# Sums of squares as pairs of float32r products, one product turned into a transposition, and a first weight tile loaded ahead of x

## Chip, cores and metric

The kernel runs as one program on one core of a Trainium2 chip. The metric is the device time of one execution in microseconds (us); a kernel is judged by the median of its runs.

## What is computed

One step of a two-layer decoder trunk for 1024 prompt rows and 64 sample rows (8 sequences of 8), side by side as 1088 columns. Layer 0 mixes by a gated delta rule (GDN, 4 heads) and a latent attention (8 heads); layer 1 by a gated linear recurrence (HGRN2, 8 heads of 128). Every mixer and every MLP is preceded by an RMS norm, and the mixers normalise per head. These are the places at which sums of squares are taken:

```
def rmsnorm(x, g):                      # over 1024 before each mixer, each MLP and at the end;
    xf = x.astype(jnp.float32)          # over 128 on each head's output
    y = xf * lax.rsqrt(jnp.mean(xf * xf, axis=-1, keepdims=True) + EPS)
    return (y * g.astype(jnp.float32)).astype(x.dtype)

def l2norm(x):                          # on q and k of each GDN head
    xf = x.astype(jnp.float32)
    return xf * lax.rsqrt(jnp.sum(xf * xf, axis=-1, keepdims=True) + EPS)
...
x = x + o
x = x + sq_relu_mlp(rmsnorm(x, mlp_norm[layer]), w_up[layer], w_down[layer])
```

## The kernel before, in words

Activations stand transposed: features on 128 partitions, the 1088 rows as columns, in three chunks of 384, 384 and 320 (`CH`). Every large product is made of three float32r products (`dense`, L335 to L337): weights and activations are each split into a high part, the value cast to float32r, and a low part, the rest (`split_pair`, L265 the cast on ACT, L266 the subtraction on DVE); high by high, high by low and low by high are added up in PSUM. Small products run on plain float32 operands.

A sum of squares over the features is a product with a 128x128 matrix of ones (`k.ones`): it leaves the sum of a column on all partitions. It stands at these places:

- The norm over 1024 features, `split_x`, one chunk at a time: ACT squares eight 128-row tiles, POOL adds the first seven into `ssa` (L286), the eighth stays in `ssl`, and `inv_rms` makes two float32 products with ones (L295), one on each. This is done for x before layer 0, before each MLP and before layer 1; the last norm (`final_norm`) has the same two products.
- `pairs` in `in_proj`, once per GDN head: six products (L695), three chunks each of k and q, one behind the other in a small pipeline of three `nq` buffers.
- The end of `core` in `hgrn`, once per HGRN2 head: three products (L1935) on `o2`, the squares of the head's output.

`attend_prompt` brings reciprocals, one per query row, onto 64 partitions each: `rcw` times the identity, a float32 product (L1454), 32 times.

Four things set the order of the work. The Python generators are woven (`weave`): the projections of the next head run between the steps of the present one (`core(h)` with `proj(h + 1)`, and `core(7)` with `out_early`). The framework then orders the instructions of each engine when the program is built, by a time model of its own. Each engine takes its instructions strictly in that order. And tiles of one tag in one pool share a fixed number of buffers: a new tile waits until the last reader of the tile that held its buffer is done. In `hgrn` the tiles `y` of the seven levels of a head, and `kd`, share the two buffers of the tag "y". In `pairs` the tags "he" and "hd" have one buffer each; `he` takes the load of `cum_d` (L712) for each group of chunks.

At the start SP and ACT load x in pairs of 128-row tiles (`load_x`, L447), two of the four for each chunk on each queue; the first weight tile `win` (L457) follows on SP, and the constants `cst`, the ones and the identity among them.

Of the kernel before, what the change touches and what calls it, by code (L numbers as in the profile page):

```python
# [13 lines left out]
ALU = mybir.AluOpType  # L14
# [157 lines left out]
def setup(k, nc, tc, A, O, ctx):  # L172
    k.nc, k.tc, k.A, k.O, k.ctx = nc, tc, A, O, ctx
    k.P = lambda name, bufs=1, **kw: tc.tile_pool(name=name, bufs=bufs, **({} if kw.get("space") == DRAM else {"reuse_waits": "tile"}), **kw)
    k.cp = ctx.enter_context(k.P("consts"))
    k.cst = k.cp.tile([128, NCST], F32, name="cst")
    k.vec = k.cp.tile([128, NVEC], F32, name="vec")
    k.eps = k.cp.tile([128, 2], F32, name="eps")
    k.rb = k.cp.tile([128, NT], F32, name="rb")
    k.dr = ctx.enter_context(k.P("dr", space=DRAM))  # L180
    nc.scalar.preload_act_table_set(EXP_SET)
    nc.gpsimd.memset(k.eps[:, 0:1], EPS)
    nc.gpsimd.memset(k.eps[:, 1:2], EPS * 128)
    C = lambda o, n, p=128: k.cst[0:p, o:o + n]
    k.ident, k.tri, k.maskT = C(C_ID, 128), C(C_TRI, 128), C(C_MT, 128)
    k.tri8, k.mk8, k.ones, k.ones8 = C(C_TRI8, 64, 64), C(C_MK8, 64, 64), C(C_ONE, 128), C(C_ONE8, 64, 64)
    k.V = lambda o: k.vec[:, o:o + 1]
# [78 lines left out]
    (eng or k.nc.vector).tensor_tensor(lo, src, hi.bitcast(F32), ALU.subtract)  # L266


def rsqrt_from(k, out, ps, scale, bias):

    nc = k.nc
    nc.scalar.activation(out, ps, AF.Ln, bias=bias, scale=scale)
    nc.scalar.activation(out, out, AF.Exp, scale=-0.5)


def squares(k, pool, x, c, n):

    nc = k.nc
    T = lambda tag, name: pool.tile([128, 384], F32, tag=tag, bufs=2, name=name)[:, :n]
    acc = t = T("ssa", f"ssa{c}")  # L280
    for kk in range(8):
        if kk:
            t = T("ssq", f"ssq{c}{kk}") if kk < 7 else T("ssl", f"ssl{c}")
        nc.scalar.activation(t, x[:, kk], AF.Square)  # L284
        if 0 < kk < 7:
            nc.gpsimd.tensor_tensor(acc, acc, t, ALU.add)  # L286
        yield acc, t


def inv_rms(k, pool, sq, c, n, r, ps):  # L290

    nc = k.nc
    p = ps()[:, :n]
    for i in range(2):
        nc.tensor.matmul(p, k.ones, sq[i], start=i == 0, stop=i == 1)  # L295
    nc.scalar.activation(r, p, AF.Ln, bias=k.eps[:, 0:1], scale=1.0 / 1024)
    nc.scalar.activation(r, r, AF.Exp, scale=-0.5)
    yield

    v, r2 = (pool.tile([128, 384], F32, tag="nwt", bufs=2, name=f"nwt{c}{i}")[:, :n] for i in range(2))  # L300
    nc.vector.tensor_scalar(v, p, -0.5 / 1024, -0.5 * EPS, ALU.mult, ALU.add)
    nc.scalar.activation(r2, r, AF.Square)
    nc.vector.tensor_tensor(v, v, r2, ALU.mult)
    nc.vector.scalar_tensor_tensor(r, v, 1.5, r, ALU.add, ALU.mult)
    yield


def split_x(k, pool, sqp, x, c, n, g_off, r, ps, xs, lag):
# [7 lines left out]
    for kk in range(8):  # L316
        nc.scalar.mul(hi[:, kk], x[:, kk], k.V(g_off + kk))
        nc.vector.scalar_tensor_tensor(lo[:, kk], x[:, kk], k.V(g_off + kk), hi[:, kk].bitcast(F32),  # L318
                                       ALU.mult, ALU.subtract)
        sq = next(s)  # L320
        yield
    for _ in range(lag):
        yield
    yield from inv_rms(k, sqp, sq, c, n, r, ps)
# [101 lines left out]
def in_proj(k):  # L426
# [16 lines left out]
    def load_x(c):  # L443
        t0, n = CH[c]
        x = xlp.tile([128, 8, 384], F32, tag="x", bufs=2, name=f"x{c}")[:, :, :n]
        for i in range(0, 8, 2):
            (nc.scalar if i % 4 else nc.sync).dma_start(x[:, i:i + 2], A["xT"][:, i:i + 2, t0:t0 + n])  # L447
        xv.append(x)


# [8 lines left out]
    def split_next():  # L459
        if raws:  # L460
            W.append(split_w(k, xp, raws.popleft(), [128, 8, 128], "w", 2))
    nc.scalar.dma_start(k.vec, A["vec"])
    load_x(0)
    load_w(xlp, "w0")
    nc.sync.dma_start(k.cst, A["cst"])
    load_x(1)
    load_w()
# [206 lines left out]
    def pairs(h, ys, z):  # L674
# [7 lines left out]
        yield  # L682
        items = [(t, t0, n) for t in (kn, q) for t0, n in CH]
        T = lambda i: rp.tile([128, 384], F32, tag="nq", bufs=3, name=f"nq{h}{i}")[:, :items[i][2]]
        r, ps = {}, {}
        for i in range(len(items) + 2):
            if i > 1:
# [4 lines left out]
            if 0 < i <= len(items):  # L692
                n = items[i - 1][2]
                ps[i - 1] = k.mm()[:, :n]
                nc.tensor.matmul(ps[i - 1], k.ones, r[i - 1], start=True, stop=True)  # L695
            if i < len(items):
                t, t0, n = items[i]
                r[i] = T(i)
                nc.scalar.activation(r[i], t[:, t0:t0 + n], AF.Square)
            yield  # L700
        nc.sync.dma_start(k.y_d[h, 1], kn)
        egl, egs = k.egl[h], k.egs[h]
# [643 lines left out]
def attend_prompt(k):  # L1346
# [76 lines left out]
    def mix(hp, qb, Ps):  # L1423
# [27 lines left out]

        rcw = T([128, 2, 64], f"rcw{hp}{qb}", tag="rcw", bufs=2)
        nc.gpsimd.tensor_copy(rcw, Ps[0][1].unsqueeze(2).broadcast_to([128, 2, 64]))
        nc.tensor.matmul(po[:, 128:256], rcw.rearrange("p j d -> p (j d)"), k.ident, start=True, stop=True)  # L1454
        tm = T([128, 128], f"to{hp}{qb}", tag="tm", bufs=2)
        ob = T([128, 128], f"ob{hp}{qb}", tag="ob", bufs=2)
        nc.scalar.copy(tm, po[:, 128:256])
# [246 lines left out]
def hgrn(k, X, before):  # L1704
# [61 lines left out]
    def core(h):  # L1766
# [150 lines left out]
        for c in range(8):  # L1917
# [12 lines left out]
            St = Sn  # L1930
            yield 0.9
        nc.sync.dma_start(O["hgrn_p"][h], St)
        for c, (t0, n) in enumerate(CH):
            p = k.sm()
            nc.tensor.matmul(p[:, :n], k.ones, o2[:, t0:t0 + n], start=True, stop=True)  # L1935
            nc.scalar.activation(o2[:, t0:t0 + n], p[:, :n], AF.Ln, bias=epsd, scale=1.0 / 128)
        nc.scalar.activation(o2, o2, AF.Exp, scale=-0.5)
        nc.vector.tensor_tensor(oz, oz, o2, ALU.mult)
# [57 lines left out]
```

## Time and profile before

| | |
|---|---|
| Runs | 3300.77 us median of 3 (3298.63 to 3304.87) |
| Profiled execution | 3298.84 us, of which the span of its instructions is 3297.1 us |
| TensorE clock granted, mean | 0.984 of full speed |
| PE busy | 3163.4 us, 96% of the span |
| DVE busy | 1709.0 us, 52% |
| ACT busy | 1107.8 us, 34% |
| POOL busy | 543.8 us, 16% |
| DMA | 288.70 MB, mean 88 GB/s |

A busy time counts an engine from the first to the last moment of each instruction; matmuls overlap, so a busy PE may still have slack. A row of the chain of waits names the work that the end of the program hung on at that time. A float32 product shows as two MATMUL records, one of float32r as one.

### The profile page before, as it was taken

To read this page: it belongs to the slowest core of one execution; us is meant where nothing else is said; L and a number is where in the kernel's file an instruction comes from. 1 tells how busy PE (TensorE), PEld (TensorE's weight loads), DVE (VectorE), ACT (ScalarE), POOL (GpSimd) and SP (SyncE) were. 2 spreads that over 40 slices of the span, in tenths; PEclk is the share of its full clock that TensorE was granted. 3 is DMA by queue.
4 is the path that set the end of the run, shared out by engine and by line. 5 is a ranking of instruction groups with operands and counts; after the bars stand their busy time and mean duration, and the time that the engine had idled before them with its cause. 6 is when DMAs were issued, how large, how long until landed. Compare 5 with 4: busy or idle time off the path is not lost. (4 is left out here: it accounts for less than half of the span.)

```text
span 3297.1 us, 63998 instructions
## 1 busy us (share of the span) xinstructions
PE 3163.4 (96%) x26944; PEld 2928.9 (89%) x26944; DVE 1709.0 (52%) x3102; ACT 1107.8 (34%) x2046; POOL 543.8 (16%) x581
## 2 busy tenths in 40 slices
PE   8999998899989999999999999999899999999997
PEld 7777875687878999999999989889799999999997
DVE  5324443665537445444546555555656444444446
ACT  5334433344415221122123445544535122212212
POOL 3021224112102000000001344443522000000002
PEclk9999999999999999999999999999899999999999
DMA  4666668422132111111112111111322111111111
GB/s 147 199 224 202 218 225 288 149 74 94 57 115 84 45 45 42 43 52 46 33 52 77 56 53 54 53 58 43 131 73 64 33 52 52 45 33 52 46 39 55
DMA packets 140279, 288.70 MB, mean 88 GB/s; under 512 B 16536, under 2 KB 85496, under 8 KB 139992
## 3 DMA queue, kind: packets, MB, share of 16 engines
q1 hardware_dynamic: 118248, 210.60, 19.4%
q10 hardware_dynamic: 12528, 40.45, 3.8%
q0 software_dynamic: 9216, 33.56, 3.1%
q8 instruction: 212, 3.47, 0.4%
q14 instruction: 75, 0.61, 0.1%
HBM read 235.48 MB, written 49.08 MB: 86 GB/s over the span
## 5 line engine op out<-in xcount | busy, mean ns | idle before, releaser
L335 PE MATMUL mm<-xh,wh 128*128 128x384 f32 (+1 forms) x2808 | 936.9, 334 | 12.4 <-ACT wh L265 11.2
L337 PE MATMUL mm<-xh,wl 128*128 128x384 f32 (+1 forms) x2808 | 929.2, 331 | 0.2 <-DVE wl L266 0.2
L336 PE MATMUL mm<-xl,wh 128*128 128x384 f32 (+1 forms) x2808 | 929.0, 331 | 0.0
L1664 DVE TENSOR_TENSOR xr<-xr,sm 128x384 f32<-128x384 f32 (+1 forms) x768 | 404.8, 531 | 430.5 <-PE sm L1663 430.4
L335 PEld LDWEIGHTS mm<-xh,wh 128*128 128x128 f32 x2808 | 531.4, 189 | 23.3 <-ACT wh L265 11.2
L337 PEld LDWEIGHTS mm<-xh,wl 128*128 128x128 f32 x2808 | 531.0, 189 | 9.5 <-issue 6.5
L336 PEld LDWEIGHTS mm<-xl,wh 128*128 128x128 f32 x2808 | 531.0, 189 | 9.1 <-issue 5.1
L1661 PE MATMUL sm<-hh,dh 128*128 128x384 f32 (+1 forms) x1536 | 505.0, 329 | 6.6 <-DVE xr L1664 5.2
L1663 PE MATMUL sm<-hh,dl 128*128 128x384 f32 (+1 forms) x1536 | 503.2, 328 | 0.0
L1662 PE MATMUL sm<-hl,dh 128*128 128x384 f32 (+1 forms) x1536 | 502.5, 327 | 0.0
L286 POOL TENSOR_TENSOR ssa<-ssa,ssq 128x384 f32<-128x384 f32 (+1 forms) x90 | 95.1, 1057 | 1725.0 <-ACT ssq L284 1722.1
L1638 ACT ACTIVATE hraw<-hraw 128x384 f32<-128x384 f32 (+1 forms) x192 | 96.9, 505 | 689.7 <-DVE hraw L1637 689.6
L1661 PEld LDWEIGHTS sm<-hh,dh 128*128 128x128 f32 x1536 | 288.8, 188 | 9.9 <-DVE xr L1664 7.5
L1662 PEld LDWEIGHTS sm<-hl,dh 128*128 128x128 f32 x1536 | 288.6, 188 | 0.6 <-issue 0.2
L1663 PEld LDWEIGHTS sm<-hh,dl 128*128 128x128 f32 x1536 | 288.7, 188 | 0.0
L1637 DVE SCALAR_TENSOR_TENSOR hraw<-mm,rb 128x384 f32<-128x384 f32 (+1 forms) x192 | 102.7, 535 | 184.6 <-PE mm L337 184.5
L265 ACT CAST dh<-dr 128x1024 fp32r<-128x1024 f32 x64 | 66.9, 1048 | 389.6 <-PE sm L1662 381.2
L266 DVE TENSOR_TENSOR hl<-hraw,hh 128x384 fp32r<-128x384 f32 (+1 forms) x192 | 102.3, 533 | 114.8 <-ACT hh L265 114.8
L265 ACT CAST wh<-wr 128x1024 fp32r<-128x1024 f32 x96 | 100.7, 1049 | 137.2 <-PE mm L336 135.3
L266 DVE TENSOR_TENSOR wl<-wr,wh 128x1024 fp32r<-128x1024 f32 x96 | 122.3, 1275 | 37.3 <-ACT wh L265 37.2
L265 ACT CAST hh<-hraw 128x384 fp32r<-128x384 f32 (+1 forms) x192 | 94.9, 494 | 5.1
L928 POOL DMA_INDIRECT lt<-in_lat,ix x64 | 67.0, 1046 | 159.1 <-PE sc L885 66.0
(659 smaller groups left out, 4522.0 us busy)
## 6 DMA issues: line engine op xcount, KB each, us to landing
la<-in_latT SPq DMA_DIRECT2D x256, 144.0 KB, 4.2
wr<-in_w_up SPq DMA_DIRECT2D x64, 512.0 KB, 3.4
dr<-in_w_down ACTq DMA_DIRECT2D x64, 512.0 KB, 4.3
wr<-in_w_in_c SPq DMA_DIRECT2D x32, 512.0 KB, 3.5
win<-in_w_in_ab SPq DMA_DIRECT2D x21, 512.0 KB, 3.9
y_d<-y SPq DMA_DIRECT2D x12, 544.0 KB, 3.1
oC_d<-g SPq DMA_DIRECT2D x8, 544.0 KB, 3.8
q_d<-q SPq DMA_DIRECT2D x16, 256.0 KB, 3.4
```

The costliest lines, as they stand in the source:

```text
L265: k.nc.scalar.copy(hi, src)
L266: (eng or k.nc.vector).tensor_tensor(lo, src, hi.bitcast(F32), ALU.subtract)
L286: nc.gpsimd.tensor_tensor(acc, acc, t, ALU.add)
L335: nc.tensor.matmul(acc, wh[:, kk], xh, start=f, stop=False)
L336: nc.tensor.matmul(acc, wh[:, kk], xl, start=False, stop=False)
L337: nc.tensor.matmul(acc, wl[:, kk], xh, start=False, stop=l)
L1637: nc.vector.scalar_tensor_tensor(raw[:, s], p[:, :n], 0.0, k.rb[:, s], ALU.max, ALU.mult)
L1638: nc.scalar.activation(raw[:, s], raw[:, s], AF.Square)
L1661: nc.tensor.matmul(p[:, :n], wh[:, m], hh[:, s], start=a, stop=False)
L1662: nc.tensor.matmul(p[:, :n], wh[:, m], hl[:, s], start=False, stop=False)
L1663: nc.tensor.matmul(p[:, :n], wl[:, m], hh[:, s], start=False, stop=b)
L1664: nc.vector.tensor_tensor(k.xr[c][:, m], k.xr[c][:, m], p[:, :n], ALU.add)
```

## The change

It adds a float32r copy of the ones, `k.onesr`, and `col_sums`, which splits a sum of squares into two products with it: one on the high part of the squares, one on the low part. In `split_x` POOL adds the eighth square too, and the whole sum is split. In `pairs` the two parts take the buffers "he" and "hd"; in `hgrn` they take the two buffers "y", and the whole of `o2` is split at once. `final_norm` keeps its float32 products. The product with the identity becomes a transposition. At the start, the first weight tile is loaded on SP ahead of x, and all four loads of x's first chunk are on SP.

```
+    k.onesr = k.cp.tile([128, 128], F32R, name="onesr")
+    nc.gpsimd.memset(k.rb[:, 0:128], 1.0)
+    nc.gpsimd.tensor_copy(k.onesr, k.rb[:, 0:128])
...
+def col_sums(k, p, hl):
+    for i in range(2):
+        k.nc.tensor.matmul(p, k.onesr, hl[i], start=i == 0, stop=i == 1)
...
-            t = T("ssq", f"ssq{c}{kk}") if kk < 7 else T("ssl", f"ssl{c}")
+            t = T("ssq", f"ssq{c}{kk}")
...
-    for i in range(2):
-        nc.tensor.matmul(p, k.ones, sq[i], start=i == 0, stop=i == 1)
+    if sq[0] is not None:
+        for i in range(2):
+            nc.tensor.matmul(p, k.ones, sq[i], start=i == 0, stop=i == 1)
+    else:
+        col_sums(k, p, sq[1])
...
+    nc.gpsimd.tensor_tensor(sq[0], sq[0], sq[1], ALU.add)
+    yield
+    hl = [sqp.tile([128, 384], F32R, tag="ss" + i, bufs=1, name=f"ss{i}{c}")[:, :n] for i in "hl"]
+    split_pair(k, *hl, sq[0])
+    sq = None, hl
...
-            (nc.scalar if i % 4 else nc.sync).dma_start(x[:, i:i + 2], A["xT"][:, i:i + 2, t0:t0 + n])
+            (nc.scalar if i % 4 and c else nc.sync).dma_start(x[:, i:i + 2], A["xT"][:, i:i + 2, t0:t0 + n])
...
+    load_w(xlp, "w0")
     load_x(0)
-    load_w(xlp, "w0")
...
+        TR = lambda i, j: rp.tile([128, 512], F32R, tag="hd" if j else "he", bufs=1, name=f"nh{h}{i}{j}")[:, :items[i][2]]
...
-                nc.tensor.matmul(ps[i - 1], k.ones, r[i - 1], start=True, stop=True)
+                col_sums(k, ps[i - 1], hl)
...
                 nc.scalar.activation(r[i], t[:, t0:t0 + n], AF.Square)
+                hl = TR(i, 0), TR(i, 1)
+                split_pair(k, *hl, r[i])
...
-        nc.tensor.matmul(po[:, 128:256], rcw.rearrange("p j d -> p (j d)"), k.ident, start=True, stop=True)
+        nc.tensor.transpose(po[:, 128:256], rcw.rearrange("p j d -> p (j d)"), k.ident)
...
+        hl2 = [hl.tile([128, NT], F32R, tag="y", bufs=2, name=f"oh{h}{i}") for i in range(2)]
+        split_pair(k, *hl2, o2)
         for c, (t0, n) in enumerate(CH):
             p = k.sm()
-            nc.tensor.matmul(p[:, :n], k.ones, o2[:, t0:t0 + n], start=True, stop=True)
+            col_sums(k, p[:, :n], [t[:, t0:t0 + n] for t in hl2])
```

Since the order is set by the framework, the change also moves instructions that the diff does not name. Three places matter here. Line numbers of the changed kernel run ahead: L265 is L268 there, L317 is L328, L335 to L337 are L351 to L353, L1773 is L1792, L1797 is L1816, L1818 is L1837.

The first is ACT at the start, from its first load on. Before (`xh` is the high part of a tile of x, `ssa` and `ssq` are squares, `wh` the high part of the first weights):

```order
L462 DMA vec<-in_vec 128x118
L447 DMA x_91<-in_xT 128x2x384 x2
L447 DMA x_99<-in_xT 128x2x384 x2
L317 ACTIVATE xh_108<-x_91,vec 128x384
L284 ACTIVATE ssa_112<-x_91 128x384
L317 ACTIVATE xh_108<-x_91,vec 128x384
L284 ACTIVATE ssq_116<-x_91 128x384
L317 ACTIVATE xh_108<-x_91,vec 128x384
L284 ACTIVATE ssq_121<-x_91 128x384
L317 ACTIVATE xh_108<-x_91,vec 128x384 x3
L601 ACTIVATE eA<-vec 128x4
L265 CAST wh<-win 128x1024
```

And now:

```order
L478 DMA vec<-in_vec 128x118
L463 DMA x_102<-in_xT 128x2x384 x2
L268 CAST wh<-win 128x1024
L617 ACTIVATE eA<-vec 128x4
L328 ACTIVATE xh_111<-x_96,vec 128x384
L292 ACTIVATE ssa_115<-x_96 128x384
```

The cast of the first weights has moved ahead of all work on x, and two loads have left the queue.

The second is ACT between two HGRN2 heads, where the tail of head 0 and the head of head 1 overlap. `o` is head 0's output squares, `x` and `y` are head 1's level tiles, L1883 the squares of one chunk of head 0. Before:

```order
L1786 ACT_TABLE_LOAD
L1786 ACTIVATE f_21105<-f_21105,lb,om 128x1088
L201 ACT_TABLE_LOAD
L1818 COPY y_21999<-k_21950 128x544
L1883 ACTIVATE o_21593<-sm 128x128
L1817 ACTIVATE x_21998<-f_21105 128x544
L1883 ACTIVATE o_21593<-sm 128x128
```

And now, from the last square of head 0 on:

```order
L1902 ACTIVATE o_21761<-sm 128x128
L1832 ACTIVATE x_22242<-x_22242 128x1088
L268 CAST oh_22004<-o_21761 128x1088
L1837 COPY y_22174<-k_22125 128x544
L1957 ACTIVATE o_21761<-sm,epsd 128x384 x2
```

Head 1's first copy into a `y` tile stood ahead of most of head 0's squares; it now stands behind the last of them and behind the cast for head 0's sums.

The third is PE where `core(6)` begins (L1773 transposes v, L1797 and, as L1816, its successor are the 32x32 tiles of the levels). Before:

```order
L1773 MATMUL sm<-cst,v_25157 64x128
L337 MATMUL mm<-xh_20586,wl 128x320
L335 MATMUL mm<-xh_20586,wh 128x320
L336 MATMUL mm<-xl_20587,wh 128x320
L1797 MATMUL sm<-q_25154,k_26000 32x32 x34
L1797 MATMUL sm<-y_26049 32x32 x34
L1797 MATMUL sm<-y_26118 32x32 x34
L337 MATMUL mm<-xh_20586,wl 128x320
```

And now:

```order
L1792 MATMUL sm<-cst,v_25360 64x128
L1816 MATMUL sm<-q_25357,k_26210 32x32 x34
L1816 MATMUL sm<-y_26259 32x32 x34
L1816 MATMUL sm<-y_26328 32x32 x34
L1816 MATMUL sm<-y_26373 32x32 x34
L351 MATMUL mm<-xh_20519,wh 128x384
```

Level tiles that had projections between them now stand in one run. From this row to the same row of head 7 PE has 172 products of `dense` before and 102 now: 82 projections have moved into the heads ahead, and 12 products of `out_early` have joined. ACT has 49 table loads in the whole program where it had 43, the six more all in `hgrn`, because exponentials of one head now stand between the sigmoids and SiLUs of the next.

## Rows read from the trace of the kernel before

**Rows 1.** Windows: stage, its length, busy time by engine, granted clock, DMA share.

```profile
core 0: us, PE busy (x) PEld busy (x) DVE busy (x) ACT busy (x) POOL busy (x), PEclk, DMA share, GB/s
45.00:500.00 455.00, 444.79 (x3216) 358.66 (x3215) 183.56 (x345) 174.26 (x345) 92.94 (x135) 0.99 0.65 210
500.00:522.00 22.00, 20.07 (x112) 13.11 (x114) 6.51 (x13) 9.70 (x24) 12.42 (x12) 0.79 0.81 262
522.00:910.00 388.00, 364.00 (x6380) 284.49 (x6376) 220.50 (x591) 160.90 (x437) 80.75 (x141) 0.97 0.38 123
1050.00:1600.00 550.00, 550.00 (x3332) 550.00 (x3331) 267.75 (x459) 118.96 (x196) 0.00 (x0) 1.00 0.14 45
1825.00:2316.00 491.00, 469.67 (x5354) 440.37 (x5353) 271.05 (x419) 230.38 (x317) 198.93 (x147) 0.99 0.15 50
2316.00:2446.00 130.00, 114.83 (x1475) 102.61 (x1474) 79.31 (x125) 54.11 (x84) 60.49 (x44) 0.91 0.29 99
```

**Rows 2.** Waits of PE, 0 to 40 us: us in total, times, longest.

```profile
PE mm L335 <- ACT wh L265: 11.2, 1, 11.2
PE mm L295 <- POOL ssa L286: 3.3, 2, 1.8
```

**Rows 3.** The chain that ended last: start, us, what (x counts MATMUL records).

```profile
2164.51 1.29 PE sm L1935 x4
...
2292.04 0.76 PE wide L1772 x7
```

**Rows 4.** Timeline of PE, 2008 to 2010 us: start, us, instruction.

```profile
2008.14 0.33 PE L335 MATMUL mm<-xh,wh 128*128 128x384 f32 x1
...
2009.18 0.34 PE L335 MATMUL mm<-xh,wh 128*128 128x384 f32 x1
2009.36 0.38 PE L1926 MATMUL sm<-AT,vt 128*128 128x128 f32 x2
...
2009.80 0.39 PE L1919 MATMUL sm<-vt,kt 128*128 128x128 f32 x2
```

**Rows 5.** Groups by line: out<-in, shapes, count, busy us, mean ns, idle before.

```profile
L265 ACT CAST hh<-hraw 128x384 fp32r<-128x384 f32 (+1 forms) x192 | 94.9, 494 | 5.1
L266 DVE TENSOR_TENSOR hl<-hraw,hh 128x384 fp32r<-128x384 f32 (+1 forms) x192 | 102.3, 533 | 114.8 <-ACT hh L265 114.8
L265 ACT CAST wh<-wr 128x1024 fp32r<-128x1024 f32 x96 | 100.7, 1049 | 137.2 <-PE mm L336 135.3 <-DMA wr<-in_w_up 1.9
L266 DVE TENSOR_TENSOR wl<-wr,wh 128x1024 fp32r<-128x1024 f32 x96 | 122.3, 1275 | 37.3 <-ACT wh L265 37.2
L286 POOL TENSOR_TENSOR ssa<-ssa,ssq 128x384 f32<-128x384 f32 (+1 forms) x90 | 95.1, 1057 | 1725.0 <-ACT ssq L284 1722.1 <-PE sm L1663 0.3
L1815 POOL TENSOR_TENSOR y<-x,q 128x512 f32<-128x512 f32 (+1 forms) x48 | 75.8, 1578 | 0.0
L1819 POOL TENSOR_TENSOR y<-x,q 128x544 f32<-128x544 f32 x8 | 17.0, 2125 | 95.7 <-ACT x L1817 95.7
L1781 ACT ACT_TABLE_LOAD x16 | 20.5, 1283 | 0.3
```

**Rows 6.** Timeline of the start, 0 to 36 us.

```profile
1.25 3.64 ACTq L447 DMA_DIRECT2D x<-in_xT  x4
...
10.08 1.03 ACT L265 CAST wh<-win 128x1024 fp32r<-128x1024 f32 x1
```

**Rows 7.** DMA issues, 0 to 30 us: count, KB each, median us to landing.

```profile
win<-in_w_in_ab SPq DMA_DIRECT2D x3, 512.0 KB, 6.9
```

**Rows 8.** Timeline of POOL, 28 to 60 us.

```profile
29.72 8.72 POOL L286 TENSOR_TENSOR ssa<-ssa,ssq 128x384 f32<-128x384 f32 x8 [1.99 <-ACT ssq L284]
```

**Rows 9.** DMA issues, 100 to 520 us.

```profile
he<-cum_d SPq DMA_DIRECT2D x7, 256.0 KB, 5.0
```

**Rows 10.** Timelines of ACT and PE, 1920 to 1960 us.

```profile
1928.34 0.67 ACT L1818 COPY y<-k 128x544 f32<-128x544 f32 x1
...
1944.35 1.45 PE L1935 MATMUL sm<-o,cst 128*128 128x384 f32 x4
```

## The prediction

> **What bounds the kernel now.** I read the busy times by stage first, then PE's waits and the chain that ended last, then single instructions. By stage PE is the bound nearly everywhere [rows 1]: in the first MLP it is busy for 550.00 of 550 us, and in the in-projection, the attention stage and the HGRN2 heads up to the seventh for 444.79 of 455, 364.00 of 388 and 469.67 of 491. Two stretches are looser: 500 to 522 us, where the in-projection's last head runs out of products, and 2316 to 2446 us, HGRN2 heads 6 and 7, with 130 − 114.83 = 15.2 us of idle PE at a clock of 0.91. At the start the first product waits 11.2 us for the cast of its weights, and two float32 sums soon after wait 3.3 us for POOL [rows 2]. So work taken from PE should count, unless something else is late at that place.
>
> **What the products cost.** A float32 sum over 384 columns takes 1.29 / 2 = 0.645 us, and seven transpositions of 128x128 take 0.76 us, 0.109 each [rows 3]. Six steps of float32r products of 384 columns take 2009.18 − 2008.14 = 1.04 us, 0.173 each, so a pair costs 0.347; two float32 products of 128 columns lie 2009.80 − 2009.36 = 0.44 us apart, 0.22 each [rows 4]. For 320 columns I scale: 0.54 and 0.289. One float32 sum replaced by a pair thus saves 0.298 us (384) or 0.249 (320).
> - Norms: before, each chunk had two float32 sums, now one pair: 1.29 − 0.347 = 0.94 us, or 0.79 for 320; 2.67 per norm, four norms 10.7.
> - `pairs`: two times (0.298 + 0.298 + 0.249) = 1.69 per head, four heads 6.8.
> - `hgrn`: 0.845 per head, eight heads 6.8.
> - Reciprocals: 32 x (0.22 − 0.109) = 3.6.
>
> PE loses 27.9 us of work in all. The Trainium skill's page "TensorE: Matmul & The Clock Gate" (Back-to-back issue gap) gives N / 2.4 + 2.5 ns per product, for 384 columns 0.1625 us, by which (an estimate) a pair would cost 0.325 and the sum would be about 1 us larger; the trace's own 0.173 is what I use.
>
> **What of it arrives, place by place.** The added work is one cast (0.49 us for 384 columns, 1.05 for 1024) and one subtraction (0.53 and 1.28) per sum, one POOL addition (1.06) per norm chunk, and six table loads of 1.28 us on ACT [rows 5].
>
> *Start and first norm.* ACT spends 3.64 us from 1.25 us on issuing four loads of x, and casts the weights only at 10.08 us, behind six tiles of x [rows 6]. Now the cast stands first. The weights go out first on SP, at about 0.76 us; landing took 6.9 us in the median [rows 7], though then behind x. With that and a cast of 1.05 us the first product starts at 8.7 instead of 11.2, 2.5 us earlier. If the tile landed at once on being issued, the gain would be up to 9 us; if x's first pair, now behind 512 KB, were as late, nothing. The median is a row of this very transfer, so I take 2.5. The sums save 2.7, and the two waits of 3.3 us go, since the sums now stand after more products. What is late next is POOL: it already runs eight additions of two chunks without a pause, 8.72 us [rows 8], and three more go in, 3.2 us, then a cast and a subtraction, 1.0 us, before the last sum. 2.5 + 2.7 + 3.3 − 3.2 − 1.0 = 4.3; I count 4, with ends 0 and 9.
>
> *The other three norms*: 3 x 2.67 = 8.0. The longer way to the sum (addition, cast, subtraction, 2.1 us) is hidden by products: PE has none idle in the MLP that follows, and a tile of 24 products lasts 24 x 0.173 = 4.2 us. If that cover were gone, 2 us per norm would return: ends 2 and 8.
>
> *Reciprocals*: 3.6, of which I count 3, as PE is busy 94% of that stage; ends 0 and 3.6.
>
> *`pairs`*: 6.8 less what its new order costs. The parts have one buffer each, so a chunk's cast waits for the chunk before to be summed, and the load of `cum_d`, which could come early into `he`, now waits for the last sum; it takes 5.0 us to land [rows 9]. For three heads projections cover this. The fourth has none left (500 to 522 us, clock 0.79), and the prompt side's first products stand behind it: 5 us for the load and about 1 us for the serial casts come onto the path. 6.8 − 6 = 1, with ends −4 (SP's queue holds cache loads up behind that load too) and 6.8.
>
> *`hgrn`*: 6.8 less two things. The sums hold both `y` buffers, so the next head's level tiles, which began at 1928.34 us, 16 us ahead of the sums at 1944.35 [rows 10], now begin after them; in heads 1 to 5 projections stand between, and I cost that at nothing. But the projections have been drawn forward, and core(6) keeps 102 products instead of 172: 70 x 0.173 = 12.1 us less cover in the stretch that was loose already. I take three quarters of it, 9 us, as idle, since head 7 is better covered at its start than before. The new table loads lie beside PE in most heads. 6.8 − 9 = −2; ends 6.8 and, with all 12.1 and six loads of 1.28 us on the path, −13.
>
> Sum: 4 + 8 + 3 + 1 − 2 = 14 us gained, against the profiled execution's 3298.84 us: 3285 us. That execution lies 1.9 us below the median of the runs shown, 3300.77, against which the chances are meant; 0.2% of it, 6.6 us, is about what a measurement of this kernel can tell from no change.
>
> **The rivals.**
> - *PE bounds everything.* All 27.9 us arrive, with 2.5 of the start and the 3.3 of waits: 3265 us. For it speaks PE's share in every long stage; against it the two loose stretches, which lie just where the order has become tighter.
> - *Both loose stretches eat more than they get.* `pairs` at its lower end (−4) and `hgrn` at its lower end (−13): 3298.8 − (4 + 8 + 3 − 4 − 13) = 3301 us, no change. For it speaks that both chains are longer and the covers thinner.
> - *The `y` buffers bind in every head, and the kernel is slower.* After a head's last square come a cast of 1.05, a subtraction of 1.28 and sums of about 1 us, and only then the next head's first `y` (2.13) and second (two multiplications of 1.58) [rows 5]; the run of level tiles on PE that needs them stands some 25 products, 4.3 us, behind the sums. If the head start of 16 us was what kept the levels in step, each of seven heads loses about 4 us: `hgrn` −2 − 28 = −30, and 3313 us. It decides as soon as PE idles over 3 us more per head there. Against it: the two runs need 5.3 us and have 4.3, which makes 1 us, not 4.
> - *The transpositions cost clock.* The granted clock in the attention stage is 0.97 [rows 1], so some 6% of 388 us, 23 us, already ran at half speed, among the transpositions of the scores. If the 32 new ones doubled that, half of 23, 12 us, would be lost: 3297 us. The trace has the stage mostly at the higher level in spite of those, which speaks against it. The same page of the Trainium skill (Part 4: PE-mode transpose) says that a transposition does not count as PE-busy for the clock in the same way as a product; by that rule this rival holds, and no row here shows it.
>
> **How the numbers follow.** The forecast 0.62, PE bounds everything 0.17, both stretches 0.12, the buffers 0.06, the clock 0.03. Faster by over 0.2% are the first two, 0.79; within it the third and most of the last, 0.14; slower 0.07. The forecast's own terms put it between 3275 and 3294. The range reaches down to 3268, which leaves half of the first rival out, and up to 3300, which leaves out half of the third case and the buffers: about 0.19 outside.
>
> **What would show it.** PE's first product at 8 to 9 us. About 28 us less of PE's own work on L295, L695, L1935 and L1454, and 120 more float32r products. The MLP stages still without idle PE. Between 500 and 540 us a wait of PE that ends with `he` from `cum_d` or DVE's `hu`. In `hgrn`, idle PE in front of the level tiles of head 6, 20 us or more in heads 6 and 7 together; in heads 1 to 5 no more than before. I am wrong if the first product starts no earlier, if the norms' sums make PE wait for POOL, or if PE idles over 3 us more per head in heads 1 to 5.

## The result, and the profile after

The change makes the kernel slower: 3341.31 us median of six runs (3331.23 to 3345.16), against 3302.07 for six of the kernel before, a ratio of 1.0116 with a 95% interval of 1.0100 to 1.0133. That is 38 us lost; the forecast was 14 gained, and its range ended at 3300. The profiled execution took 3345.16 us, the longest of the six; the one before took 3298.84, so the two traces compared below lie 46 us apart. What a run gains or loses in us is worked out from its ratio and the median of the kernel before.

PE has less to do, and yet is busy 9.6 us longer than before (3163.4). Its mean granted clock went from 0.984 to 0.969: it ran more often at the lower of its two levels. Page, kernel after:

```profile
PE 3173.0 (95%) x26888; PEld 2949.5 (88%) x26888; DVE 1759.4 (53%) x3146; ACT 1138.3 (34%) x2096; POOL 559.1 (17%) x595
```

Where the time went is read from the starts of the same instructions in both traces. Difference, after less before:

| place | before | after | difference |
|---|---|---|---|
| first product | 11.2 | 7.4 | -3.8 |
| layer 0's scores, first product (L878) | 93.7 | 94.5 | +0.8 |
| attention stage, first product (L1404) | 589.4 | 594.0 | +4.6 |
| out-projection, first product | 928.9 | 930.4 | +1.5 |
| first MLP, first down product (L1661) | 1092.5 | 1091.9 | -0.6 |
| HGRN2, transposition of head 0 (L1773) | 1868.5 | 1872.6 | +4.1 |
| second MLP, first down product | 2557.3 | 2604.9 | +47.6 |

Up to HGRN2 nothing is gained or lost beyond a few us. HGRN2 loses 43.5. One window for that stage in each kernel (columns as in [rows 1]), kernel before first:

```profile
1868.50:2557.30 688.80, 649.69 (x7203) 605.62 (x7202) 405.29 (x638) 322.96 (x489) 276.26 (x208) 0.98 0.19 65
```

Kernel after, with the first MLP above it:

```profile
1050.00:1600.00 550.00, 550.00 (x3333) 550.00 (x3332) 268.72 (x461) 119.30 (x196) 0.00 (x0) 1.00 0.14 45
1872.60:2604.90 732.30, 661.44 (x7197) 622.75 (x7195) 436.06 (x649) 340.65 (x506) 280.87 (x211) 0.93 0.18 61
```

Idle PE in HGRN2 grew from 39 us (688.8 - 649.7) to 71 (732.3 - 661.4), and the granted clock fell from 0.98 to 0.93. The MLP is as full as in [rows 1]. What the engines of HGRN2 waited for in the kernel after, POOL first, then PE (us in total, times, longest):

```profile
POOL y L1838 <- PE sm L274: 203.7, 6, 35.3
...
PE sm L1856 <- POOL y L1834: 15.3, 5, 6.7
PE mm L351 <- DVE g L1781: 12.3, 3, 6.9
PE sm L1816 <- POOL y L1834: 5.0, 2, 3.3
```

POOL's first `y` of six heads waits for the sums of the head before, up to 35.3 us. Before, it waited at this place for ACT's `x`, of the same head as `y`:

```profile
POOL y L1819 <- ACT x L1817: 95.7, 6, 43.5
```

The end of head 1 shows it one instruction at a time. Timelines of PE, ACT, DVE and POOL, kernel after (start, length; in brackets the idle time before and its releaser):

```profile
2023.09 0.39 PE L1947 MATMUL sm<-qg,S 128*128 128x128 f32 x2
...
2023.52 0.28 ACT L1902 ACTIVATE o<-sm 128x128 f32<-128x128 f32 x1 [0.65 <-PE sm L1947]
2023.82 1.11 ACT L268 CAST oh<-o 128x1088 fp32r<-128x1088 f32 x1
...
2025.18 1.29 DVE L269 TENSOR_TENSOR oh<-o,oh 128x1088 fp32r<-128x1088 f32 x1
...
2028.35 0.66 PE L274 MATMUL sm<-oh,onesr 128*128 128x384 f32 x3
...
2029.05 0.70 ACT L1837 COPY y<-k 128x544 f32<-128x544 f32 x1 [2.35 <-PE sm L274]
...
2029.09 1.62 POOL L1838 TENSOR_TENSOR y<-x,q 128x544 f32<-128x544 f32 x1 [34.84 <-PE sm L274]
...
2030.47 1.47 ACT L1957 ACTIVATE o<-sm,epsd 128x384 f32<-128x384 f32 x3 [0.71 <-PE sm L274]
```

The same place before:

```profile
1995.83 0.68 ACT L1818 COPY y<-k 128x544 f32<-128x544 f32 x1
...
2014.09 0.39 PE L1928 MATMUL sm<-qg,S 128*128 128x128 f32 x2
2015.21 0.81 PE L1935 MATMUL sm<-o,cst 128*128 128x384 f32 x2
```

Two things are new. From the last output product to the first sum it was 1.1 us, and is 5.3: square, cast and subtraction, done at 2026.47, and then PE is among projections for 1.9 us more. And the next head's first `y`, which came 18 us ahead of the last output product, now comes 6 us behind it.

### The profile page after: what moved, and what is told of

Its sections match the earlier page's. It is cut to its first block, busy times and chain, and to the rows that moved or that the text cites. A ratio compares the mean times of both kernels' runs of the same rounds, so it can differ in the third digit from the quotient of the medians.

```text
span 3343.4 us, 64075 instructions
## 1 busy us (share of the span) xinstructions
PE 3173.0 (95%) x26888; PEld 2949.5 (88%) x26888; DVE 1759.4 (53%) x3146; ACT 1138.3 (34%) x2096; POOL 559.1 (17%) x595
## 4 chain that ended last, share of the span: by engine, by line
PE 70%; DVE 6%; issue 2%; ACT 2%; DMA 2%; POOL 2%; SPq 0%; DVEq 0%; ACTq 0%; POOLq 0%
PE mm L353 12%; PE mm L352 12%; PE mm L351 12%; PE sm L1680 7%; PE sm L1682 7%; PE sm L1681 7%; DVE xl L329 1%; PE po L1452 1%; PE tr L1460 1%; POOL y L1834 1%; PE mm L1077 1%; DVE x L1830 1%; PE sc L1423 1%; DVE f L1839 1%; POOL y L1833 1%
## 5 line engine op out<-in xcount | busy, mean ns | idle before, releaser
L351 PE MATMUL mm<-xh,wh 128*128 128x384 f32 (+1 forms) x2808 | 939.1, 334 | 23.4 <-DVE g L1781 12.3
L353 PE MATMUL mm<-xh,wl 128*128 128x384 f32 (+1 forms) x2808 | 932.9, 332 | 3.7 <-DVE wl L269 3.7
L351 PEld LDWEIGHTS mm<-xh,wh 128*128 128x128 f32 x2808 | 537.4, 191 | 35.5 <-DVE g L1781 12.8
L352 PEld LDWEIGHTS mm<-xl,wh 128*128 128x128 f32 x2808 | 536.6, 191 | 10.3 <-issue 4.6
L353 PEld LDWEIGHTS mm<-xh,wl 128*128 128x128 f32 x2808 | 536.9, 191 | 8.0 <-DVE wl L269 4.2
L268 ACT CAST dh<-dr 128x1024 fp32r<-128x1024 f32 x64 | 66.9, 1048 | 381.2 <-PE sm L1681 380.9
L268 ACT CAST wh<-wr 128x1024 fp32r<-128x1024 f32 x96 | 100.8, 1050 | 129.4 <-PE mm L352 126.9
L268 ACT CAST hh<-hraw 128x384 fp32r<-128x384 f32 (+1 forms) x192 | 95.0, 495 | 5.2
L1839 DVE TENSOR_TENSOR f<-f 128x512 f32<-128x512 f32 (+1 forms) x56 | 74.9, 1337 | 41.1 <-ACT x L1836 23.1
```

What stands on the lines that cost most here:

```text
L268: k.nc.scalar.copy(hi, src)
L351: nc.tensor.matmul(acc, wh[:, kk], xh, start=f, stop=False)
L352: nc.tensor.matmul(acc, wh[:, kk], xl, start=False, stop=False)
L353: nc.tensor.matmul(acc, wl[:, kk], xh, start=False, stop=l)
L1839: nc.vector.tensor_tensor(up(f), up(f), tot, ALU.add)
```

## Experiments

Theory A: the sums hold both `y` buffers, and the next head cannot start ahead. Theory B: HGRN2 only shows a loss made elsewhere. Theory C: the added casts and subtractions delay what stands behind them on ACT and DVE. Theory D came up with the first four results: the sums wait for the split, PE takes its instructions in order, and the next head stands behind the sums.

### Which part

```
-        hl2 = [hl.tile([128, NT], F32R, tag="y", bufs=2, name=f"oh{h}{i}") for i in range(2)]
-        split_pair(k, *hl2, o2)
         for c, (t0, n) in enumerate(CH):
             p = k.sm()
-            col_sums(k, p[:, :n], [t[:, t0:t0 + n] for t in hl2])
+            nc.tensor.matmul(p[:, :n], k.ones, o2[:, t0:t0 + n], start=True, stop=True)
```

> The changed kernel with the HGRN2 sums of squares put back to float32 products; norms, pairs, transpositions and the start stay changed. Theory A (the y buffers: each head's sums hold both buffers that the next head's level tiles need): the 43 us that the HGRN2 heads lost come back, 3341 - 43 = 3298 us, with HGRN2 heads 1 to 6 at about 74 us each again. Theory B (the loss is in the clock or the start, and HGRN2 only shows it): less than 15 us come back, 3326 us or more. In either case the stages before HGRN2 end within 5 us of the kernel before, as in the changed kernel.

Measured: 3296.71 us, ratio 0.9982 (0.9966 to 0.9998). B is out: without the HGRN2 part the other parts make the kernel 6 us faster. The reverse, the HGRN2 part alone on the kernel before:

> The kernel before with the HGRN2 sums alone changed. Theory A: slower by about the 43 us that the HGRN2 heads lost in the changed kernel, less what the barer seventh head cost there (it keeps 157 products here, 102 there; 55 x 0.173 = 9.5 us): 3302 + 34 to 43 = 3336 to 3345 us. Theory B: within 15 us of the kernel before.

Measured: 3337.62 us, ratio 1.0099 (1.0076 to 1.0123). So this part alone costs 33 us, and all of it lies in HGRN2 (732.2 us for the stage, against 688.8).

### Which mechanism

The parts in buffers that are free at the head's end, in the kernel after and alone:

```
-        hl2 = [hl.tile([128, NT], F32R, tag="y", bufs=2, name=f"oh{h}{i}") for i in range(2)]
+        hl2 = [hl.tile([128, NT], F32R, tag="qg", bufs=1, name=f"oh{h}"),
+               hl.tile([128, 9, 128], F32R, tag="kt", bufs=1, name=f"ol{h}").rearrange("p c t -> p (c t)")[:, :NT]]
```

> The changed kernel, with the two parts of the HGRN2 squares in the buffers of qg and kt, whose last readers are done at the head's end, in place of the two y buffers. Cast, subtraction, sums and table loads stay. Theory A: POOL's first y of a head no longer waits for the sums (203.7 us in the changed kernel), PE's waits for y fall back to some 8 us, and the time to 3341 - 43 - up to 6.8 of saved sums = 3291 to 3298 us. Theory C (the split's own work on ACT and DVE, in front of the projections' copies out of PSUM, makes the loss): the wait of PE for DVE's copies stays at some 12 us, and 3325 us or more.

> The kernel before with the HGRN2 sums alone changed, and the parts in the buffers of qg and kt. Theory A: the 6.8 us of saved sums arrive at best, 3295 to 3302 us. Theory C: over 3325 us, as with the y buffers.

Measured: 3327.28 us, ratio 1.0068 (1.0044 to 1.0091), and 3334.00, ratio 1.0093 (1.0067 to 1.0120). A alone is not enough: POOL's wait for the sums is gone and the stage is 21 and 17 us shorter than with the `y` buffers, but 22 and 26 us of loss remain. These numbers are those that C named, and D had not been stated yet. The next four tell C and D apart.

> The kernel before with the cast and the subtraction of the HGRN2 squares added (into the buffers of qg and kt), but nothing reads them: the sums stay float32 products of the squares. Theory C (the added 2.3 us of ACT and DVE per head delay what stands behind them on those engines): most of the 22 to 26 us that the HGRN2 heads lost with free buffers stay, 3322 us or more. Theory D (the sums wait for the split, PE takes its instructions in order, and the next head and the out-projection stand behind the sums): without that wait the time is that of the kernel before plus 0 to 7 us, 3304 to 3311 us.

> The kernel before with the HGRN2 sums alone changed, parts in the buffers of qg and kt, cast and subtraction both on POOL, which is slower at them than ACT and DVE. Theory C: ACT and DVE are rid of the added work, so faster than the 3334 us of the same with ACT and DVE by 15 us or more. Theory D: the sums wait longer than 2.3 us after the last square, so as slow or slower, 3334 to 3350 us.

> The kernel before with one float32r product on the cast squares in each HGRN2 sum; the low part of the squares is left out. The sums wait for the cast alone, 1.05 us in place of 2.33, and PE saves 11.3 us rather than 6.8. Theory C (DVE's subtraction is the worse half): back to 3304 us or less. Theory D: some half of the loss stays, 3304 + 12 - 4 = 3312 us, 3306 to 3320.

> The kernel before with float32 HGRN2 sums, and both y buffers held until they are done: ACT copies 8 columns of the squares into each, and two products of 8 columns, whose result nobody reads, take them up behind the last sum. Theory A (holding y costs by itself): the 17 to 21 us by which the HGRN2 heads lost more with y than with free buffers, 3321 to 3325 us. Theory D (the long way to the sums does it, the buffers only add where both meet): within 7 us of the kernel before, 3311 us at most.

Their edits, in this order; the first three are made in the kernel with the HGRN2 part alone and free buffers (in the third `hl2` is one tile, in the buffer of `qg`), the last in the kernel before:

```
         split_pair(k, *hl2, o2)
...
-            col_sums(k, p[:, :n], [t[:, t0:t0 + n] for t in hl2])
+            nc.tensor.matmul(p[:, :n], k.ones, o2[:, t0:t0 + n], start=True, stop=True)
...
-        split_pair(k, *hl2, o2)
+        nc.gpsimd.tensor_copy(hl2[0], o2)
+        nc.gpsimd.tensor_tensor(hl2[1], o2, hl2[0].bitcast(F32), ALU.subtract)
...
-        split_pair(k, *hl2, o2)
+        nc.scalar.copy(hl2, o2)
...
-            col_sums(k, p[:, :n], [t[:, t0:t0 + n] for t in hl2])
+            nc.tensor.matmul(p[:, :n], k.onesr, hl2[:, t0:t0 + n], start=True, stop=True)
...
+        hold = [hl.tile([128, NT], F32, tag="y", bufs=2, name=f"oh{h}{i}") for i in range(2)]
+        for t in hold:
+            nc.scalar.copy(t[:, 0:8], o2[:, 0:8])
...
+            if c == 2:
+                for t in hold:
+                    nc.tensor.matmul(p[:, 376:384], k.ones, t[:, 0:8], start=True, stop=True)
```

Measured: work unread 3294.11 us, ratio 0.9974 (0.9958 to 0.9989); split on POOL 3355.84, 1.0177 (1.0149 to 1.0206); cast only 3316.51, 1.0053 (1.0030 to 1.0077); `y` held 3339.80, 1.0133 (1.0101 to 1.0166). C falls as the cause of the main loss: the same work costs nothing when nothing waits for it. It was not put off to a quieter place, either: in work unread the cast begins 0.9 to 2.2 us behind a head's last output product, with free buffers alone 0.8 to 2.2 in seven heads and 4.0 in one. (That it came out below the kernel before, and below D's range, no theory here explains; of the 8.5 us between the two profiled executions 5.4 lie in the in-projection and the attention stage, where its instructions are those of before.) Taking the work off ACT and DVE makes it worse; that run says less, since POOL takes 1.44 and 2.62 us in the mean for the cast and the subtraction. D holds in both directions: a shorter wait costs less, a longer one more. A holds too, and more than expected: held buffers alone, with hardly any work, cost 44 us by the ratio, 36 by the medians, 39 in the stage. That POOL then waits for the sums shows in that kernel's row:

```profile
POOL y L1819 <- PE sm L1941: 234.4, 7, 35.9
```

The HGRN2 stage (window from head 0's transposition to the second MLP) of work unread, cast only, split on POOL and `y` held:

```profile
1863.60:2550.00 686.40, 650.86 (x7203) 607.18 (x7201) 420.04 (x646) 330.94 (x497) 273.46 (x208) 0.98 0.20 65
```

```profile
1870.20:2574.20 704.00, 651.26 (x7180) 611.57 (x7179) 400.01 (x638) 334.55 (x500) 269.52 (x208) 0.95 0.19 64
```

```profile
1867.20:2602.60 735.40, 657.07 (x7203) 618.56 (x7202) 415.20 (x638) 331.78 (x496) 300.94 (x224) 0.94 0.18 61
```

```profile
1864.60:2592.00 727.40, 671.79 (x7235) 627.43 (x7233) 425.78 (x638) 325.99 (x505) 287.29 (x208) 0.94 0.18 62
```

The two mechanisms act at two places of a head. Means over the heads, from the starts of each head's transposition (L1773), last output product (L1926) and first Ln (L1936), in us:

| kernel | transposition to last output product | last output product to Ln | last output product to next transposition | stage |
|---|---|---|---|---|
| before | 65.5 | 3.4 | 6.8 | 688.8 |
| work unread | 65.1 | 4.2 | 7.8 | 686.4 |
| cast only | 66.4 | 6.0 | 9.2 | 704.0 |
| alone, free buffers | 65.9 | 7.4 | 10.7 | 714.8 |
| split on POOL | 66.9 | 10.3 | 12.3 | 735.4 |
| `y` held | 69.9 | 3.0 | 6.7 | 727.4 |
| alone, `y` buffers | 68.2 | 7.6 | 11.3 | 732.2 |
| after | 68.4 | 7.6 | 10.5 | 732.3 |

A wait for the split lengthens the gap between heads; held `y` buffers lengthen the inside of a head. In the kernel after this is 8 x 2.9 + 7 x 3.7 = 49 us; the stretch from head 7's last output product to the second MLP gives 5.7 back (117.0 before, 111.3 after). The gap is longer between all heads, by 1.0 to 4.6 us. The inside is not: heads 4, 5 and 7 carry 5.9, 10.8 and 5.6 us of its 23, the others 2.4 at most, while with `y` held alone every head but the first is 3.4 to 6.5 us longer. The two do not add up either: 26 us (free buffers) and 39 (`y` held) in the stage by themselves, 43 together.

Two things stay open. PE itself hardly stands for the split: its wait for `oh` is 0.3 us in the whole program (row L274 `sm<-oh,onesr` below). The delay is in the order, made by the framework's time model, which has projections ahead of the sums: in seven heads of the kernel after they begin 1.5 to 2.3 us after the subtraction is done, with the cast alone 3.0 to 3.5 us after the cast. How much of D is the split and how much an order with more room than the split needs, no run here separates. And the new table loads on ACT are not told apart from D: the kernels whose sums wait for a whole split or cast have 46 to 50 of them, those without that wait (before, work unread, `y` held and the last test below) 43. At 1.28 us each [rows 5] they are 4 to 9 us of ACT, against 15 to 47 us lost in those stages, and with `y` held there are none more.

A split that nobody waits for should then keep the saved products. The last test makes it in pieces of 128 columns, each behind its square:

```
-            nc.scalar.activation(o2[:, s], p, AF.Square)
+            sq = hl.tile([128, 128], F32, tag="osq", bufs=1, name=f"osq{h}{s.start}")[:, :s.stop - s.start]
+            nc.scalar.activation(sq, p, AF.Square)
+            split_pair(k, his if s.start == SEQ else hi[:, s], lo[:, s], sq)
```

> The kernel before with the HGRN2 sums alone changed, but the split made in pieces of 128 columns (64 for the samples), each right behind its square: the high parts go into the buffer of S0, the low parts into that of o2, the squares of a piece into one small buffer, and the result of Ln into that of qg. So when the last square is done only a cast and a subtraction of 128 columns stand before the last sum, and the y buffers are not touched. Theory D: the loss goes and the saved products come in as far as PE was the bound: 3303 less 0 to 7 us, 3296 to 3303. Theory C (the split's work itself, which is more here, nine casts and subtractions a head): 3320 us or more.

Measured: 3311.88 us, ratio 1.0024 (1.0009 to 1.0038): 9 us above D's range and 8 below C's, so neither named it. The stage takes 693.5 us, which is within the 684.9 to 696.3 that it takes in the nine kernels here that leave HGRN2 as it was; the gap is 6.9 as before, and the inside of a head 67.0, 1.5 more than before. With both waits gone most of the loss is gone, and the saved products have brought nothing. What the remaining 8 us are is open; the nine casts and subtractions of each head may be a part of them.

### The other parts

> The kernel before with the first weights ahead of x and the transpositions, no other part. The forecast's terms: the first product 2.5 us earlier by the forecast, 3.8 as the changed kernel's profile has it, and 3 us in the attention stage: 6 us faster, 3297. Rival: PE waits for a later tile of x or of weights instead and the clock falls at the start, and only the 3 us stay, 3300.

> The kernel before with the norms' sums alone changed. The forecast's terms: 8 us from three norms and some 1.5 from the first, 3294 us. Rival (the sums wait for POOL's last addition, the cast and the subtraction wherever the norm follows products closely, as in the changed kernel's profile at 1808 and 1813 us, and the clock falls with it): no gain, 3300 to 3306.

> The kernel before with the sums of the GDN heads alone changed. The forecast's term: 1 us faster, 3302, with 6.8 us of products gone and 6 lost between 500 and 540 us. Rival: no wait for the load behind the buffer there, 3297. Other rival: 4 us slower, 3307.

Each is one part of the change's diff, put alone into the kernel before. Measured: start and transpositions 3291.39 us, ratio 0.9979 (0.9964 to 0.9993); norms 3307.17, 1.0016 (1.0004 to 1.0027); pairs 3288.64, 0.9965 (0.9950 to 0.9980). The start and the transpositions give what was expected. The norms cost 5 us instead of giving 10. Rows of the kernel with the norms alone: PE's wait in the first 60 us, its wait for the sums at the norm behind the first MLP (in the kernel before, then in this one), and the timelines there:

```profile
PE mm L353 <- DVE wl L269: 3.9, 2, 3.6
```

```profile
PE sm L295 <- POOL ssa L286: 1.3, 1, 1.3
PE sm L274 <- ACT ssh L268: 5.0, 2, 3.2
```

```profile
1803.05 1.00 POOL L333 TENSOR_TENSOR ssa<-ssa,ssq 128x384 f32<-128x384 f32 x1 [0.67 <-ACT ssq L292]
...
1805.48 0.50 ACT L268 CAST ssh<-ssa 128x384 fp32r<-128x384 f32 x1
...
1806.03 0.29 PEld L274 LDWEIGHTS sm<-ssh,onesr 128*128 128x128 f32 x1 [3.55 <-ACT ssh L268]
```

At the start PE no longer waits for POOL, but 3.6 us for the low part of the second weight tile. At 1802.8 us PE has come to the sum of a chunk while POOL is still adding, and ACT casts behind other work; it waits over 3 us, and its granted clock is 0.50, the lower of its levels, from 1805.5 to 1808.9 us. By the starts of the first table this kernel is 2.2 us behind at layer 0's scores, and from the first down product to HGRN2 it takes 779.1 us, where each of the twelve kernels that leave the norms alone takes 776.0 or 776.1: 3.1 us lost at the norm before HGRN2. The two places of the other norms, -1.5 us up to the first down product and +2.4 in the HGRN2 stage, lie within what kernels with these stages unchanged differ by. Four more runs: start, transpositions and pairs together; the same without the transpositions; and, to see whether POOL's addition or the split is late, the kernel before with the eighth square added on POOL and one float32 product in place of two, with no split; and that edit together with the three parts. The edit:

```
+    nc.gpsimd.tensor_tensor(sq[0], sq[0], sq[1], ALU.add)
+    sq = sq[:1]
...
-    for i in range(2):
-        nc.tensor.matmul(p, k.ones, sq[i], start=i == 0, stop=i == 1)
+    for i, t in enumerate(sq):
+        nc.tensor.matmul(p, k.ones, t, start=i == 0, stop=i == len(sq) - 1)
```

> The changed kernel without its HGRN2 part and without its norms part: start, transpositions and pairs. If the three parts add up by their own stages: the start gives 1 to 3 us, the transpositions 3, the pairs 3 to 7, in all 7 to 13 us: 3290 to 3296. If the gains of the two runs before were theirs in full, 11 + 14: 3278. If they were the luck of the attention stage's order: 3295 to 3303.

> Start and pairs without the transpositions. If the transpositions are worth 3 us of products: 3 us slower than the run with all three. If the attention stage's order sets its length, whatever the transpositions save: anywhere within 10 us of it, with a stage of 329 to 346 us as in the other runs.

> The kernel before, where POOL adds the eighth square in the norms too and the sum is one float32 product in place of two; no cast, no subtraction, no float32r. PE saves 0.645 us a chunk (12 chunks, 7.3 us with the narrower ones). If the split, queued on ACT and DVE behind the work on later tiles, makes the sums late: 3296 to 3300 us. If POOL's addition alone does: no gain, 3303 to 3308.

> Start, transpositions, pairs, and the norms by one float32 product. If one product is the better norm: 3 to 7 us below the run without it. If POOL's addition makes the sums late: the same or up to 5 us slower.

Measured: start, transpositions and pairs 3288.10 us, ratio 0.9962 (0.9948 to 0.9976); without the transpositions 3291.97, 0.9978 (0.9967 to 0.9989); one product in the norms 3307.20, 1.0014 (1.0003 to 1.0025); that with the three 3298.28, 0.9990 (0.9981 to 1.0000). So with POOL's addition alone the norms lose as much as with the split, though a product is saved. How, is not shown: from the first down product to HGRN2 that kernel takes 778.2 us, but PE's wait for POOL at the norm there is 1.3 us, as before. **Start, transpositions and pairs beat both kernels**, by 12.5 us the one before and by some 50 the one after.

The three gains do not add up (7 + 12 against 12.5), and where they lie can't be settled here. Much of them shows in the attention stage, whose length wanders. Its window in the kernel before, and in the kernels with the HGRN2 part alone, `y` and free buffers, whose PE instructions up to HGRN2 are the same and, but for two pairs of neighbours, in the same order:

```profile
589.40:928.90 339.50, 308.37 (x6093) 244.43 (x6091) 199.71 (x564) 148.35 (x413) 61.36 (x116) 0.96 0.31 99
```

```profile
588.20:921.10 332.90, 302.00 (x6094) 239.45 (x6092) 199.24 (x564) 148.82 (x413) 61.28 (x116) 0.98 0.31 101
```

```profile
585.50:931.10 345.60, 313.85 (x6093) 248.45 (x6091) 200.22 (x564) 149.47 (x413) 61.28 (x116) 0.93 0.30 98
```

The same instructions take 332.9 to 345.6 us, and the clock goes with it (0.98, 0.96, 0.93). In the eight kernels that differ in HGRN2 alone, the kernel before among them, the out-projection starts between 921.1 and 931.6 us, and 491.5 to 495.8 us lie between the first scores and the attention: so much a single profile can say of a part that touches only these stages. The runs with gains had 329.8 (pairs), 330.4 (start and transpositions) and 335.5 (all three). The part with pairs reorders this stage too, so luck of the execution and effect of the order can't be separated by one profile each.

## Why the prediction was wrong

**The step that failed** is `hgrn`: "in heads 1 to 5 projections stand between, and I cost that at nothing". The term was -2, with -13 as its lower end; it is -43.5 in the stage. The later start of the level tiles was seen, with its 16 us, and so was the barer end; both were priced as PE time left uncovered. But the heads are a chain. PE meets the sums, the next transposition and the level tiles in a fixed order, and the projections in between were already set to fill the gaps of the old chain. What lengthens the chain by 1 us is paid once per head, though PE is 95% busy [rows 1]. The projections that PE takes meanwhile are then missing in head 6: it has 102 products instead of 172, and its idle time, transposition to transposition, went from 6.9 to 18.9 us. This was the one part of the term that was near: 9 us forecast, 12.0 measured.

The rival "the `y` buffers bind in every head" named half of the mechanism, at 0.06, and its price, 4 us per head, was near: held buffers alone cost 4.4 inside a head (69.9 - 65.5). What spoke against it, 5.3 us needed and 4.3 there, counted instructions and not the order. No rival had the other half, that the sums come later, behind the split and more projections, and that the next head stands behind them. The forecast's mark for this, over 3 us more idle per head in heads 1 to 5, was passed narrowly, and in the mean alone: 33.9 us in place of 16.7, most of it in heads 4 and 5. Idle PE is 32 of the 43.5 us. The rest is the clock, which the forecast had left out for this stage: PE's busy time there rose by 11.7 us (661.4 - 649.7) although its sums had become 6.8 us shorter.

**Norms** was the second: 8 us counted for three norms, since "PE has none idle in the MLP that follows"; the part cost 5 us. The full window lies behind the norm. At the norm itself PE stood for the way over POOL and ACT, 5.0 us before HGRN2 (that the norms' sums make PE wait for POOL was listed as a mark of error), and with POOL's addition alone the loss was as large.

**Start**: the first product came at 7.4 us, where 8.7 was forecast:

```profile
0.75 0.40 SPq L473 DMA_DIRECT2D win<-in_w_in_ab  x1
...
4.89 1.04 ACT L268 CAST wh<-win 128x1024 fp32r<-128x1024 f32 x1 [2.85 <-DMA win<-in_w_in_ab]
...
7.35 0.69 PE L351 MATMUL mm<-xh,wh 128*128 128x384 f32 x1 [7.35 <-ACT xh L328]
```

The weights landed 4.1 us after the issue, not 6.9. What was gained is gone by 50.7 us, to the wait for the second weights. **Reciprocals**: right in size as far as it can be seen: the attention stage takes 335.9 us in the mean of the six kernels with transpositions and 338.8 in that of the twelve without, 2.9 less, forecast 3, though single ones differ by more; start and transpositions together gave 7, forecast 2.5 + 3, and the run without the transpositions was 4 us slower than the same with them (3291.97, 3288.10), forecast 3. **`pairs`**: forecast 1, measured 12 (7 to 16). The wait for the load of `cum_d` hardly came onto the path: between 495 and 600 us of the kernel after PE waits 2.8 us for the split (`nh`) and 1.8 for `hu`, none for the load itself, and with pairs alone not for `hu` either. Where the 12 us lie is open; the stage up to the attention takes 492.6 us with pairs alone, which is within the spread above. PE's own work on sums and reciprocals fell by 24 us, not 28 (77.1 to 53.2, the groups of these lines added up). What is missing lies in `pairs`, whose sums became only 0.7 us shorter: a product takes 399 ns on average there, where I had scaled from products in a row, 173 each. Groups by line, before and after:

```profile
L695 PE MATMUL mm<-nq,cst 128*128 128x384 f32 (+1 forms) x48 | 18.1, 472 | 0.0
L1935 PE MATMUL sm<-o,cst 128*128 128x384 f32 (+1 forms) x48 | 17.5, 470 | 0.0
```

```profile
L274 PE MATMUL mm<-nh,onesr 128*128 128x384 f32 (+1 forms) x48 | 17.4, 399 | 2.9 <-DVE nh L269 2.8
L274 PE MATMUL sm<-oh,onesr 128*128 128x384 f32 (+1 forms) x48 | 10.7, 331 | 0.3 <-DVE oh L269 0.3
```

**The transpositions cost clock**: not shown, and no time was lost. The Trainium skill's page "TensorE: Matmul & The Clock Gate" (Part 4: PE-mode transpose) says that a transposition does not count as busy for the clock in the same way as a product. The granted clock of the attention stage was 0.92 to 0.96 in the six kernels with the 32 transpositions, 0.94 in the mean, and 0.93 to 0.98 in the twelve without, 0.95 in the mean. That points the way of the rule, by less than the same instructions differ from run to run, and the stage is shorter all the same. The stage with start and transpositions, and with start and pairs:

```profile
586.10:916.50 330.40, 300.15 (x6062) 238.45 (x6060) 197.77 (x564) 147.87 (x413) 60.54 (x116) 0.96 0.31 102
```

```profile
592.10:926.30 334.20, 305.89 (x6093) 243.76 (x6091) 198.95 (x563) 148.10 (x412) 60.49 (x116) 0.96 0.31 100
```

## What to carry to other kernels

A stage in which PE is 95% busy can still be a chain: look for what each iteration's last step waits for and which buffers it holds, and price what you put there once per iteration. Before a sum is moved to a cheaper product, count how long its operands take to get there, and try the parts alone: here three of them together were worth 12 us, and the other two cost more than that. Where the order is set by a program, look at what filled the gaps before, because it will be drawn to the new gap and be missing later.

## What the hardware showed

In HGRN2 waits and the lower clock came together. With 35.5, 39.1, 52.7, 55.6, 70.9 and 78.3 us of idle PE in that stage (work unread, before, cast only, `y` held, after, split on POOL) the granted clock was 0.98, 0.98, 0.95, 0.94, 0.93 and 0.94. The windows of work unread and of `y` held hold the same projections, and PE is busy 21 us longer in the second (671.79 against 650.86). That the idle time alone sets the clock is not shown: in the attention windows above it is the same (30.9 to 31.8 us), at 0.93 to 0.98.

And an instruction of DVE can grow manyfold beside POOL. DVE, POOL and PE in head 5 of the kernel after, then DVE and the first and last of POOL's run of five in head 2:

```profile
2278.49 4.11 DVE L1830 TENSOR_TENSOR x<-f 128x512 f32<-128x512 f32 x1
...
2277.67 1.79 POOL L1896 TENSOR_TENSOR vx<-vt,cst 64x512 f32<-64x512 f32 x1 [0.88 <-ACT vt L1794]
2279.43 1.33 POOL L1833 TENSOR_TENSOR y<-x,k 128x544 f32<-128x544 f32 x1
2280.73 1.32 POOL L1834 TENSOR_TENSOR y<-x,q 128x544 f32<-128x544 f32 x1
...
2286.77 0.69 PE L351 MATMUL mm<-xh,wh 128*128 128x384 f32 x1 [6.91 <-DVE g L1781]
```

```profile
2036.89 6.59 DVE L1839 TENSOR_TENSOR f<-f 128x512 f32<-128x512 f32 x1
...
2035.93 1.93 POOL L1896 TENSOR_TENSOR vx<-vt,cst 64x512 f32<-64x512 f32 x1 [0.89 <-ACT vt L1794]
...
2041.68 1.24 POOL L1834 TENSOR_TENSOR y<-x,q 128x512 f32<-128x512 f32 x1
```

`x` takes 0.73 us in the median and 4.11 here: it ends 0.55 us after POOL's run of three, which ends at 2282.05. DVE's copy of a projection out of PSUM comes some instructions behind it, and PE waits 6.9 us for that. `f`, with the same median, takes 6.59 and ends 0.55 us after a run of five. All 45 instructions of DVE on `x` and `f` that last over 2.5 us, in all kernels here, end 0.55 to 0.58 us after an instruction of POOL, the last of its run. In the HGRN2 stage there are six, seven and seven of them with held buffers (after, alone with `y` buffers, `y` held) and one to four in the other kernels; so it goes with the held buffers; how much of their cost it makes is not measured. The Trainium skill's "GPSIMD Engine Reference" (1. Specifications) says that POOL shares its SBUF interfaces with VectorE, with contention for instructions of DVE with two SBUF inputs, as both of these have; the trace agrees, and has the size.
